# Squares of eight RMS norms around the output projection summed on GpSimd, with one product with the ones each

## The chip, the cores and the metric

One NeuronCore of a Trainium2 chip runs the kernel. The metric is the device time of one execution in microseconds, the median of several runs. The engines are TensorE (PE; its weight loads are PEld), VectorE (DVE), ScalarE (ACT), GpSimd (POOL) and SyncE (SP), each with an instruction queue that it works off in order; they hand over to each other by semaphores. Transfers are issued from the queues of SP, ACT and POOL.

## The reference

One decoder layer over 1024 prompt tokens and 32 sample tokens (8 sequences of 4, with a paged cache of 2048 positions each), float32, model width 1024:

```python
x = x + 0.5 * SwiGLU_1(rms_norm(x, g_ffn1))
q, k, v, logf, bg, uc = combined_projection(rms_norm(x, g_mix), w_in, b_f)
o_attn = forgetting_attention(q, k, v, logf)          # 8 heads of 64
conv_out = bg * short_conv(uc)                        # 512 channels
x = x + concat([rms_norm(o_attn, g_ao), rms_norm(conv_out, g_co)]) @ w_out
x = x + 0.5 * SwiGLU_2(rms_norm(x, g_ffn2))
y = rms_norm(x, g_final)

def rms_norm(x, g):
    return x * rsqrt(mean(x * x, axis=-1) + EPS) * g
```

## The kernel before, in words

Activations lie transposed: channels on the 128 partitions, tokens along the columns. The 1056 tokens are cut into four chunks `c` of 264 columns (`CH`). A tile of `[128, 4, 264]` holds four blocks of 128 channels of a chunk, so a norm over 512 channels has one such tile and a norm over 1024 channels two. Products are made in three float32r products of a high and a low part (`mm3`, lines 104 to 106).

An RMS norm (`norm`) needs, for each token, the sum of the squares over the channels, that is over the partitions and over the blocks. A product with a 128x128 matrix of ones gives that sum on all partitions at once, in a PSUM bank `ps`. `norm` has two ways to it:

- `stat_pe` (`short=True`): for each block ScalarE writes the squares of 128x264 to a small tile `sq` (tag `m1`, two buffers) and PE multiplies it with the ones in float32, adding up in `ps`. Four products for a norm over 512, eight for one over 1024.
- `stat_sum` (`short=False`): ScalarE squares a whole tile into `d` (tag `d`, one buffer), VectorE adds its halves (528 columns), then quarters (264 columns), and PE makes two float32r products of the sum's high and low part.

After that `rstd` makes 1/root of it (sqrt on ScalarE, line 170, with a table load where the table was another; reciprocal on VectorE, line 171), `scale` multiplies each block on VectorE (line 190), and `parts` makes the high part on ScalarE (line 193) and the low part on VectorE (line 194) that the next products read.

The norms that the change touches, in order of time:

- `conv_norm(0)` and `conv_norm(1)` within the attention, after its round 9 (`CONV_AT`), with banks of the attention's pool (`pco`). The order of the attention on PE is written out by hand: `front` (logits, lines 1126 to 1129, then softmax on VectorE and ScalarE), `middle` (transposes, line 1145), `back` (products with the values, line 1159; the result `at` is copied by ScalarE and VectorE, lines 1162 and 1163, and stored by a DMA from GpSimd's queue, line 1164).
- `attn_norm(0)`, `attn_norm(1)` and `conv_norm(2)` as hooks of the first half of the output projection, `project((0, 1), ...)`: it makes the products with the conv half (operand `opc`) for three blocks of the output, calls the hook, then makes those with the attention half (operand `op`) and adds `x` on VectorE (line 1263). At its end x goes to HBM by DMAs from GpSimd's queue (line 1266).
- `prepare(1)` as a hook of the second half, `project((2, 3), ...)`, and `prepare(2)` and `prepare(3)` after it. These are norms over 1024 channels; `halves` and `blocks` (lines 207 to 237) then make the operands for the next feed-forward stage, with a tile `d` of the same tag and one buffer. That stage begins with `plain` for three columns of weights, which reads operands of chunks 0 and 1 alone.

From the output projection on, a scheduler of the framework sets the order of each engine's instructions. `conv_norm(3)`, `attn_norm(2)`, `attn_norm(3)` and `prepare(0)` use `stat_sum`, before and after.

Of the kernel before, what the change touches and what calls it, by code (L numbers as in the profile page):

```python
# [8 lines left out]
F32 = mybir.dt.float32  # L9
# [3 lines left out]
AF = mybir.ActivationFunctionType  # L13
# [5 lines left out]
P = 128  # L19
D = 1024  # L20
# [11 lines left out]
CH = 264  # L32
# [26 lines left out]
G_F1, G_MIX, G_F2, G_FIN, G_AT, G_CO, CW = 0, 8, 16, 24, 32, 36, 40  # L59
# [3 lines left out]
class Step:  # L63
# [74 lines left out]
    def stat_pe(self, xs, ps):  # L138
        nc = self.nc
        for n, x in enumerate(xs):  # L140
            sq = self.tmp.tile([P, x.shape[1]], F32, tag="m1", bufs=2, name="sq")
            nc.scalar.activation(sq, x, AF.Square)
            nc.tensor.matmul(ps, self.ones, sq, start=n == 0, stop=n == len(xs) - 1)  # L143

    def stat_sum(self, ts, ps):

        nc = self.nc
        acc = None
        for t in ts:
            d = self.tmp.tile([P, 4, CH], F32, tag="d", bufs=1, name="d")  # L150
            nc.scalar.activation(d, t, AF.Square)
            nc.vector.tensor_add(d[:, 0:2], d[:, 0:2], d[:, 2:4])
            if acc is None and len(ts) > 1:
                acc = self.small("m5", self.nrs)
                nc.vector.tensor_add(acc, d[:, 0], d[:, 1])
                continue
            nc.vector.tensor_add(d[:, 0], d[:, 0], d[:, 1])
            if acc is None:
                acc = d[:, 0]
            else:  # L160
                nc.vector.tensor_add(acc, acc, d[:, 0])
        ah, al = (self.tmp.tile([P, CH], F32R, tag="m1", bufs=2, name=n) for n in ("ah", "al"))
        self.parts(ah, al, acc)
        nc.tensor.matmul(ps, self.ones_r, ah, start=True, stop=False)
        nc.tensor.matmul(ps, self.ones_r, al, start=False, stop=True)
# [8 lines left out]
    def norm(self, ts, col, n, ps=None, short=True, then=None):  # L174

        ps = self.bank() if ps is None else ps
        if short:
            self.stat_pe([t[:, k, :] for t in ts for k in range(4)], ps)
        else:
            self.stat_sum(ts, ps)  # L180
        rs = self.rstd(ps, n)
        for i, t in enumerate(ts):
            for k in range(4):
                c = col + 4 * i + k
                self.scale(t[:, k, :], t[:, k, :], self.prm[:, c:c + 1], rs)
                if then and k % 2:
                    then(i, k - 1)
# [241 lines left out]
def kernel(ctx: ExitStack, tc: tile.TileContext, io: dict):  # L429
    nc = tc.nc  # L430
    K = Step(tc, io)
# [6 lines left out]
    def pool(es, name, side="right", **kw):  # L438
        return es.enter_context(tc.tile_pool(name=name, bufs=1, side=side, reuse_waits="tile", **kw))
# [177 lines left out]
    with ExitStack() as es:  # L617
# [280 lines left out]
        def keep(g):  # L898

            po, M = ptr.tile([P, 512], F32, tag="tr", name="po"), Ms[g]  # L900
            for b4 in range(4):
                nc.tensor.transpose(po[:, P * b4:P * b4 + P], M[:, P * b4:P * b4 + P], ident)
            rows = po.rearrange("p (b a c q) -> p b a c q", b=4, a=NHP, c=4)
            for b4 in range(4):
                b = 4 * g + b4
                for hh in range(2):
                    pr = slice(HD * hh, HD * hh + HD)
                    nc.vector.tensor_copy(atS[pr, :, NT * b:NT * b + NT],
                                          rows[pr, b4, :, b4, NT * hh:NT * hh + NT])
# [176 lines left out]
    with ExitStack() as es:  # L1086
# [6 lines left out]
        def conv_load(c, pool_, tag, queue):  # L1093
            co = pool_.tile([P, 4, CH], F32, tag=tag, bufs=1, name="co")
            for t in range(4):
                queue.dma_start(co[:, t, :], co_d[t][:, c * CH:(c + 1) * CH])
            return co

        def conv_norm(c, co, ps=None):

            cs = slice(c * CH, (c + 1) * CH)
            K.norm([co], G_CO, 512, ps, short=c < 3)
            hi, lo = (opc.tile([P, 4, CH], F32R, tag=f"op{14 + 4 * c + j}", bufs=1, name="opc")
                      for j in range(2))
            K.parts(hi, lo, co)
            xo[c] = [(hi[:, k, :], lo[:, k, :]) for k in range(4)]
# [86 lines left out]
        for r in range(len(rounds)):  # L1193
            front(r + 1)
            middle(r)
            back(r - 1)
            if r == CONV_AT - 4:
                cos = [conv_load(c, K.tmp, f"co{c}", nc.gpsimd) for c in range(NCH // 2)]
            if r == CONV_AT:
                for c in range(NCH // 2):  # L1200
                    conv_norm(c, cos[c],
                              ptr.tile([P, 512], F32, tag="tr", bufs=3, name="pco")[:, :CH])
# [15 lines left out]
    def xtile(c):  # L1218

        ps, bufs = (xp0, 2) if c == 0 else (xp, 6)  # L1220
        return [ps.tile([P, 4, CH], F32, tag="x", bufs=bufs, name="x") for _ in range(2)]

    with ExitStack() as es:
        K.tmp = pool(es, "t3")
        xp = pool(es, "x3")
        xa, xs = [None] * NCH, [None] * NCH

        def attn_norm(c):

            cs = slice(c * CH, (c + 1) * CH)  # L1230

            a = op_l.tile([P, 4, CH], F32, tag=f"op{4 + c}", bufs=1, name="a")
            for t in range(NHP):
                nc.sync.dma_start(a[:, t, :], at_d[t][:, cs])
            K.norm([a], G_AT, 512, short=c < 2)
            hi, lo = (K.op_tile((16, 20, 24, 8)[c] + j) for j in range(2))
            K.parts(hi, lo, a)
            xa[c] = [(hi[:, k, :], lo[:, k, :]) for k in range(4)]

        def load_x(c):  # L1240
            xs[c] = xtile(c)
            for i in range(2):
                nc.sync.dma_start(xs[c][i], x_d[c][:, 4 * i:4 * i + 4, :])

        def project(cs, hooks):

            for (d0, d1), hook in zip(((0, 3), (3, 6), (6, KD)), hooks):
                os_ = {}
                for d in range(d0, d1):
                    ws = K.weight(io["w_out"][d, :, 512:], 512)  # L1250
                    for c in cs:
                        os_[d, c] = K.bank()
                        K.dot(os_[d, c], ws, xo[c], stop=False)
                hook()
                for d in range(d0, d1):
                    ws = K.weight(io["w_out"][d, :, :512], 512)
                    if d == 0:
                        for c in cs:
                            load_x(c)
                    for c in cs:  # L1260
                        o, x = os_[d, c], xs[c][d // 4][:, d % 4, :]
                        K.dot(o, ws, xa[c], start=False)
                        nc.vector.tensor_add(x, o, x)
            for c in cs:
                for i in range(2):
                    nc.gpsimd.dma_start(x2_d[c][:, 4 * i:4 * i + 4, :], xs[c][i])

        def prepare(c):
            K.norm(xs[c], G_F2, D, short=c > 0)
            K.halves(c // 2, c % 2, *xs[c], ops[c // 2])  # L1270

        def keep():
            K.plain_part([xp0.tile([P, 4, CH], F32R, tag="x", bufs=2, name="xb") for _ in range(2)], ops[0])

        def norms(c):
            conv_norm(c, conv_load(c, op_l, f"op{8 + c}", nc.sync))
            attn_norm(c)

        project((0, 1), (lambda: (attn_norm(0), attn_norm(1)), lambda: norms(2), lambda: norms(3)))
        project((2, 3), (lambda: prepare(0), lambda: prepare(1), lambda: K.blocks(0, ops[0], keep)))  # L1280
        w1, w3 = io["w1b"], io["w3b"]
        prepare(2)
        prepare(3)
        K.blocks(1, ops[1])
    K.after = None
# [126 lines left out]
```

## Time and profile before

| | |
|---|---|
| Median of three runs | 2158.63 us (2155.1 to 2159.55) |
| The profiled execution | 2156.09 us |
| Its span, first to last instruction | 2154.3 us |
| Mean granted clock of PE | 0.984 |
| PE busy | 2067.7 us, 96% |
| DVE busy | 1348.8 us, 63% |
| ACT busy | 866.0 us, 40% |
| POOL busy | 332.0 us, 15% |

All times within the execution are microseconds from its first instruction. PE's records overlap, since a product drains while the next one enters: the distance from start to start is what a product costs. Names at an arrow are tiles, without their buffer numbers: `ps<-sq,ones` is a product into a bank `ps` that reads `sq` and `ones`. A float32 product shows as two passes, so `x4` at line 143 is two products. The output projection runs from about 1311 to 1431.

### The profile page before, as it was taken

The numbers are of one execution on the slowest core, as the hardware profiler recorded it, in microseconds if no ns is written. First come the engines' busy times: TensorE is split into PE (matmuls) and PEld (weight loads), VectorE is DVE, ScalarE is ACT, GpSimd is POOL, SyncE is SP. The second block draws the span as 40 slices with busy tenths as digits, with TensorE's granted clock in tenths as the row PEclk, the third lists the DMA queues.
The fourth block names the chain that finished last, engine by engine and source line by source line (L and its number), as shares of the span: only waits on it lengthen the run. The fifth ranks groups of instructions, "written<-read, shape, count | busy, mean of one in ns | idle before, by whom it ended". The sixth has DMA issues, their size and how long they took to land.

```text
span 2154.3 us, 44569 instructions
## 1 busy us (share of the span) xinstructions
PE 2067.7 (96%) x17570; PEld 1981.6 (92%) x17570; DVE 1348.8 (63%) x2610; ACT 866.0 (40%) x1736; POOL 332.0 (15%) x487
## 2 busy tenths in 40 slices
PE   7999999999958999999999899999999999999998
PEld 7999999999957988888998677999999999999997
DVE  8877777776524664213225775897677677775354
ACT  6533333445312433222114764553333333454343
POOL 0011111110222021443432330001010111100000
PEclk9999999999978999999999999999999999999999
DMA  6222223257534668997976444332222222496353
GB/s 213 79 98 85 85 87 100 87 176 237 191 103 119 229 220 275 378 334 254 294 246 161 114 112 161 129 104 88 77 80 74 86 85 85 144 308 214 110 180 131
DMA packets 139618, 341.03 MB, mean 158 GB/s; under 512 B 30000, under 2 KB 46592, under 8 KB 137872
## 3 DMA queue, kind: packets, MB, share of 16 engines
q1 hardware_dynamic: 82704, 218.15, 31.6%
q0 software_dynamic: 28736, 88.50, 12.3%
q10 hardware_dynamic: 27968, 31.54, 4.8%
q8 instruction: 138, 2.26, 0.5%
q14 instruction: 72, 0.59, 0.1%
HBM read 279.75 MB, written 58.33 MB: 157 GB/s over the span
## 4 chain that ended last, share of the span: by engine, by line
PE 54%; DVE 4%; DMA 2%; ACT 1%; issue 1%; POOL 0%; SPq 0%; ACTq 0%; DVEq 0%; POOLq 0%
PE ps L105 12%; PE ps L104 12%; PE ps L106 11%; PE pg L104 4%; PE pg L105 4%; PE pg L106 4%; PE pv L886 1%; PE sc L843 1%; PE O L1159 1%; DMA wraw<-in_w_out 1%; PE ptp L1145 1%; PE S L1126 1%; PE ps L143 0%; PE S L1127 0%; ACT Pr L1134 0%
## 5 line engine op out<-in xcount | busy, mean ns | idle before, releaser
L105 PE MATMUL ps<-op,wh 128*128 128x264 f32 x2604 | 741.0, 285 | 0.7 <-DVE op L194 0.5
L106 PE MATMUL ps<-op,wl 128*128 128x264 f32 x2604 | 738.2, 284 | 0.0
L104 PE MATMUL ps<-op,wh 128*128 128x264 f32 x2604 | 737.4, 284 | 0.8 <-ACT op L193 0.4
L87 ACT CAST wh<-wraw 128x512 fp32r<-128x512 f32 x542 | 316.0, 601 | 491.3 <-PE ps L105 271.1
L104 PEld LDWEIGHTS ps<-op,wh 128*128 128x128 f32 x2604 | 489.5, 188 | 1.6 <-ACT op L193 0.8
L105 PEld LDWEIGHTS ps<-op,wh 128*128 128x128 f32 x2604 | 489.1, 188 | 1.8 <-DVE op L194 1.5
L106 PEld LDWEIGHTS ps<-op,wl 128*128 128x128 f32 x2604 | 490.2, 188 | 0.2
L89 DVE TENSOR_TENSOR wl<-wraw,wh 128x512 fp32r<-128x512 f32 x542 | 350.7, 663 | 201.8 <-ACT wh L87 176.5
L106 PE MATMUL ps<-h,wl 128*128 128x264 f32 x1408 | 405.3, 288 | 17.2 <-DVE wl L89 17.2
L105 PE MATMUL ps<-h,wh 128*128 128x264 f32 x1408 | 406.5, 289 | 14.3 <-DVE h L194 11.9
L104 PE MATMUL ps<-h,wh 128*128 128x264 f32 x1408 | 408.2, 290 | 4.5 <-ACT wh L87 4.5
L106 PEld LDWEIGHTS ps<-h,wl 128*128 128x128 f32 x1408 | 271.2, 193 | 18.7 <-DVE wl L89 18.6
L105 PEld LDWEIGHTS ps<-h,wh 128*128 128x128 f32 x1408 | 270.8, 192 | 15.2 <-DVE h L194 15.0
L104 PEld LDWEIGHTS ps<-h,wh 128*128 128x128 f32 x1408 | 271.2, 193 | 5.2 <-ACT wh L87 5.0
L104 PE MATMUL pg<-XH,wh 128*128 128x352 f32 x576 | 189.8, 329 | 1.7 <-issue 1.7
L106 PE MATMUL pg<-XH,wl 128*128 128x352 f32 x576 | 185.0, 321 | 0.3 <-issue 0.3
L105 PE MATMUL pg<-XL,wh 128*128 128x352 f32 x576 | 184.7, 321 | 0.0
L87 ACT CAST wh<-s 128x512 fp32r<-128x512 f32 x176 | 108.2, 618 | 120.3 <-PE ps L105 110.2
L89 DVE TENSOR_TENSOR wl<-s,wh 128x512 fp32r<-128x512 f32 x176 | 120.6, 690 | 24.2 <-ACT wh L87 18.9
L327 POOL DMA_DIRECT2D h_d<-t x79 | 42.8, 542 | 602.1 <-DVE t L326 598.0
L104 PEld LDWEIGHTS pg<-XH,wh 128*128 128x128 f32 x576 | 108.0, 188 | 18.4 <-issue 18.1
L106 PEld LDWEIGHTS pg<-XH,wl 128*128 128x128 f32 x576 | 108.1, 188 | 0.8 <-issue 0.8
(276 smaller groups left out, 2586.4 us busy)
## 6 DMA issues: line engine op xcount, KB each, us to landing
wraw<-in_w2a SPq DMA_DIRECT2D x48, 512.0 KB
wraw<-in_w2b SPq DMA_DIRECT2D x48, 512.0 KB
h_d<-t POOLq DMA_DIRECT2D x176, 132.0 KB
h<-h_d SPq DMA_DIRECT2D x88, 264.0 KB
kvraw<-in_kc SPq DMA_DIRECT2D x64, 256.0 KB
kvraw<-in_vc SPq DMA_DIRECT2D x64, 256.0 KB
wraw<-in_w1a SPq DMA_DIRECT2D x28, 512.0 KB
wraw<-in_w3a SPq DMA_DIRECT2D x28, 512.0 KB
```

The lines of the kernel that those rows point to most:

```text
L87: nc.scalar.copy(wh, x)
L89: nc.vector.tensor_sub(wl, x, wh)
L104: nc.tensor.matmul(ps, w[0], x[0], start=start, stop=False)
L105: nc.tensor.matmul(ps, w[0], x[1], start=False, stop=False)
L106: nc.tensor.matmul(ps, w[1], x[0], start=False, stop=stop)
L327: nc.gpsimd.dma_start(h_d[2 * p + 1][:, f, :], t)
L843: nc.tensor.matmul(ps[quarter(hp)], QZ[:, g, hp, 32 * b4:32 * b4 + 32], raw[:, :, hp * P:hp * P + P], start=b4 == 0, stop=b4 == 3)
L886: nc.tensor.matmul(pv[quarter(hp), cs], PT[:, 4 * j + s, quarter(hp)], raw[:, s, hp * P:hp * P + P], start=j == 0 and s == 0, stop=False)
L1126: nc.tensor.matmul(S[:, k0:k1], QA[:, qs], KA[:, k0:k1], start=True, stop=False)
L1145: nc.tensor.transpose(pt_[:, j * P:(j + 1) * P], Pr[:, (j0 + j) * P:(j0 + j + 1) * P], ident)
L1159: nc.tensor.matmul(O[HD * b + q:HD * b + q + 32], V[:, j, c0 + q:c0 + q + 32], pt[:, j, :], start=j == 0, stop=j == n)
```

## The change

A third way, `stat_pool`, takes the place of `stat_pe` in the eight norms. It squares a whole tile of four blocks at once on ScalarE into `d`, adds on GpSimd in float32 (halves, then quarters; with two tiles also the second tile's sum to the first's, `acc`), and makes one float32 product with the ones. The norm of chunk 1 at the kernel's start stays with `stat_pe`.

```diff
+    def stat_pool(self, ts, ps):
+
+        nc = self.nc
+        acc = None
+        for t in ts:
+            d = self.tmp.tile([P, 4, CH], F32, tag="d", bufs=1, name="d")
+            nc.scalar.activation(d, t, AF.Square)
+            nc.gpsimd.tensor_add(d[:, 0:2], d[:, 0:2], d[:, 2:4])
+            if acc is None and len(ts) > 1:
+                acc = self.tmp.tile([P, CH], F32, tag="m1", bufs=2, name="acc")
+                nc.gpsimd.tensor_add(acc, d[:, 0], d[:, 1])
+                continue
+            nc.gpsimd.tensor_add(d[:, 0], d[:, 0], d[:, 1])
+            if acc is None:
+                acc = d[:, 0]
+            else:
+                nc.gpsimd.tensor_add(acc, acc, d[:, 0])
+        nc.tensor.matmul(ps, self.ones, acc, start=True, stop=True)
+
...
-        if short:
+        if short == "pool":
+            self.stat_pool(ts, ps)
+        elif short:
             self.stat_pe([t[:, k, :] for t in ts for k in range(4)], ps)
...
-            K.norm([co], G_CO, 512, ps, short=c < 3)
+            K.norm([co], G_CO, 512, ps, short="pool" if c < 3 else False)
...
-            K.norm([a], G_AT, 512, short=c < 2)
+            K.norm([a], G_AT, 512, short="pool" if c < 2 else False)
...
-            K.norm(xs[c], G_F2, D, short=c > 0)
+            K.norm(xs[c], G_F2, D, short="pool" if c > 0 else False)
```

The lines of the changed kernel lie 19 to 21 further on: 151 is the new square, 152, 155, 157 and 161 the adds, 162 the product, 1185 the store of `at`, 1287 that of x.

What it does to the order, at two places. The first is `prepare(2)` and `prepare(3)` at the end of the output projection. On PE, before (the first row ends the projection, `op_17905` and `op_17906` belong to `plain` of the next stage):

```order
L106 MATMUL ps<-op_17709,wl 128x264
L143 MATMUL ps<-sq,ones 128x264 x9
L104 MATMUL ps<-op_17905,wh 128x264
L105 MATMUL ps<-op_17906,wh 128x264
L106 MATMUL ps<-op_17905,wl 128x264
L104 MATMUL ps<-op_17905,wh 128x264
L143 MATMUL ps<-sq,ones 128x264 x2
L105 MATMUL ps<-op_17906,wh 128x264
L143 MATMUL ps<-sq,ones 128x264 x2
L106 MATMUL ps<-op_17905,wl 128x264
L143 MATMUL ps<-sq,ones 128x264 x2
L104 MATMUL ps<-op_17905,wh 128x264
```

and now (`op_17870` and `op_17871` are the same two operands):

```order
L106 MATMUL ps<-op_17674,wl 128x264
L162 MATMUL ps<-acc,ones 128x264 x2
L104 MATMUL ps<-op_17870,wh 128x264
L105 MATMUL ps<-op_17871,wh 128x264
L106 MATMUL ps<-op_17870,wl 128x264
```

Sixteen products, the last seven of them strewn among products of the next stage, became two that stand side by side ahead of that stage. On GpSimd's queue at the same place (lines 152 to 161 are the adds, `x_d` the stores of x at the end of the projection's second half):

```order
L1287 DMA x_d_81<-x 128x1056
L1287 DMA x_d_82<-x 128x1056
L152 TENSOR_TENSOR d<-d 128x528
L1287 DMA x_d_81<-x 128x1056
L1287 DMA x_d_82<-x 128x1056
L155 TENSOR_TENSOR acc<-d 128x264
L152 TENSOR_TENSOR d<-d 128x528
L157 TENSOR_TENSOR d<-d 128x264
L161 TENSOR_TENSOR acc<-acc,d 128x264
L152 TENSOR_TENSOR d<-d 128x528
L155 TENSOR_TENSOR acc<-d 128x264
L152 TENSOR_TENSOR d<-d 128x528
```

The stores of the first halves of x of chunks 2 and 3 stand ahead of `prepare(2)`'s first add, those of the second halves between its first and second add; before, the four stores were alone there.

The second place is round 9 of the attention, `conv_norm(0)` and `conv_norm(1)`. GpSimd's queue before (`at_d` are the stores of the attention's results, `vt`, `KA` and the like loads for the next heads):

```order
L1164 DMA at_d_115<-at 64x256 x2
L1164 DMA at_d_116<-at 64x256
L926 DMA vt<-v_d_109 128x1024
L921 DMA KA<-k_d_103 64x1024 x2
L921 DMA QA<-q_d_95 64x1024
```

and now:

```order
L1185 DMA at_d_115<-at 64x256 x2
L152 ISA
L152 TENSOR_TENSOR d<-d 128x528
L1185 DMA at_d_116<-at 64x256
L157 TENSOR_TENSOR d<-d 128x264
L947 DMA vt<-v_d_109 128x1024
L152 TENSOR_TENSOR d<-d 128x528
L157 TENSOR_TENSOR d<-d 128x264
L942 DMA KA<-k_d_103 64x1024 x2
L942 DMA QA<-q_d_95 64x1024
```

The first norm's two adds stand on both sides of the third store, the second norm's after the load of `vt`; ahead of the first add stands an instruction that was not there. On PE the eight products of these two norms became two in the same place.

## Rows read from the trace of the kernel before

**Rows 1.** Page, engines: busy us, share of the span, instructions.

```profile
PE 2067.7 (96%) x17570; PEld 1981.6 (92%) x17570; DVE 1348.8 (63%) x2610; ACT 866.0 (40%) x1736; POOL 332.0 (15%) x487
```

**Rows 2.** Timeline, prepare(1): start, us, engine, line, out<-in, count [idle before <-releaser].

```profile
1381.21 0.42 ACT L142 ACTIVATE sq<-x 128x264 f32<-128x264 f32 x1 [0.20 <-PE ps L164]
...
1395.15 0.28 PE L106 MATMUL ps<-opc,wl 128*128 128x264 f32 x1
1395.27 1.05 PE L143 MATMUL ps<-sq,ones 128*128 128x264 f32 x4
1395.97 0.48 PE L104 MATMUL ps<-op,wh 128*128 128x264 f32 x1
1396.28 0.28 PE L105 MATMUL ps<-op,wh 128*128 128x264 f32 x1
...
1400.90 0.29 PE L105 MATMUL ps<-op,wh 128*128 128x264 f32 x1
```

**Rows 3.** Timeline, conv norms 0 and 1 in the attention.

```profile
1202.54 0.53 POOL L1164 DMA_DIRECT2D at_d<-at  x1 [3.26 <-DVE at L1163]
...
1204.62 1.16 PE L143 MATMUL pco<-sq,ones 128*128 128x264 f32 x4
...
1207.04 0.53 POOL L1164 DMA_DIRECT2D at_d<-at  x1 [3.96 <-DVE at L1163]
...
1211.47 0.59 PE L1126 MATMUL S<-KA,QA 128*128 128x512 f32 x1
```

**Rows 4.** Timeline, attention norms 0 and 1.

```profile
1320.23 3.06 PE L143 MATMUL ps<-sq,ones 128*128 128x264 f32 x10
...
1326.64 0.29 PE L106 MATMUL ps<-opc,wl 128*128 128x264 f32 x1
...
1329.53 1.21 DVE L194 TENSOR_TENSOR op<-a,op 128x1056 fp32r<-128x1056 f32 x1
```

**Rows 5.** Timeline, conv norm 2.

```profile
1345.20 1.05 PE L143 MATMUL ps<-sq,ones 128*128 128x264 f32 x4
...
1347.82 0.29 PE L104 MATMUL ps<-op,wh 128*128 128x264 f32 x1
```

**Rows 6.** Timeline, prepare(2) and prepare(3).

```profile
1420.07 4.35 PE L143 MATMUL ps<-sq,ones 128*128 128x264 f32 x14
...
1420.44 1.25 DVE L194 TENSOR_TENSOR op<-d,op 128x1056 fp32r<-128x1056 f32 x1
...
1423.50 0.53 POOL L1266 DMA_DIRECT2D x_d<-x  x1 [18.89 <-DVE x L1263]
...
1430.93 0.28 PE L106 MATMUL ps<-op,wl 128*128 128x264 f32 x1
```

**Rows 7.** Line 143: PE passes, duration ns min/median/max, first and last start.

```profile
L143 PE MATMUL ps<-sq,ones x88: 383/386/807, 12.2 to 1430.6; 128*128 128x264 f32 x88
```

**Rows 8.** Groups by shape: count | busy us, mean ns | idle before, releasers.

```profile
L170 ACT ACTIVATE rs<-ps,eps 128x264 f32<-128x264 f32 x22 | 10.5, 478 | 4.7 <-issue 1.6 <-PE ps L143 1.2 <-PE ps L350 0.8
L151 ACT ACTIVATE d<-x 128x1056 f32<-128x1056 f32 x8 | 8.7, 1083 | 4.9 <-DVE m L155 1.7 <-DMA x<-in_xT 1.6 <-issue 1.5
L170 ACT ACT_TABLE_LOAD x6 | 7.7, 1283 | 0.1
...
L152 DVE TENSOR_TENSOR d<-d 128x528 f32<-128x528 f32 x11 | 7.7, 701 | 8.0 <-ACT d L151 8.0
L157 DVE TENSOR_TENSOR d<-d 128x264 f32<-128x264 f32 x7 | 2.9, 420 | 0.0
...
L629 POOL MEMSET QZ<- 128x1280 f32 x1 | 1.2, 1184 | 0.0
L634 POOL MEMSET VS<- 128x512 f32 x1 | 0.5, 544 | 0.0
```

**Rows 9.** Stretches: length, busy of PE, PEld, DVE, ACT, POOL, granted clock, DMA, GB/s.

```profile
1217.00:1218.00 1.00, 0.00 (x0) 0.00 (x0) 1.00 (x1) 1.00 (x4) 0.39 (x1) 1.00 0.94 184
...
1220.00:1221.00 1.00, 1.00 (x8) 0.79 (x5) 1.00 (x2) 0.67 (x2) 0.00 (x0) 0.50 1.06 229
```

## The prediction

> **What bounds the kernel.** I read the page's engine table first: TensorE (PE) is busy 96% of the span [rows 1]. So a microsecond counts where PE stands still or does work that could go away. Then I read, place by place, what the squares cost PE. The stretch from the first product with the ones to where the ordinary products run undisturbed again, less 0.12 us for each ordinary one in between (their distance, 1395.15 to 1395.27 [rows 2]), is PE's loss to a norm. Two products back to back take 0.70 us, 0.35 each, and the ordinary one behind them 0.31 instead of 0.12 [rows 2]; the rest is waiting, since a square can be written only when a product has freed one of two buffers.
>
> - A, conv norms 0 and 1 inside the attention: 1204.62 to 1211.47, nothing in between, 6.85 us [rows 3].
> - B, attention norms 0 and 1: 1320.23 to 1326.64, five ordinary ones, 5.8 us [rows 4].
> - C, conv norm 2: 1345.20 to 1347.82, three, 2.26 us [rows 5].
> - E, prepare(1): 1395.27 to 1400.90, ten, 4.4 us [rows 2].
> - D, prepare(2) and (3): 1420.07 to 1430.93, eight, 9.9 us [rows 6].
>
> Together 29.2 us. That is the most that a free sum could give back, less 8 times 0.35 us. What matters is whether the new sum is ready when PE arrives, for PE takes its instructions in order.
>
> **The change, part by part.** *Removed:* 44 squares of 264 columns and 44 fp32 products, each two passes of 0.386 us [rows 7]. *Added:* 11 squares of 1056 columns at 1.083 us [rows 8], 8 products, 25 adds on GpSimd (11 of 528 columns, 14 of 264), and one ISA instruction ahead of the first add. ScalarE gets less to do (44 squares against 11), so only order and waits matter there. One load of x goes ahead of one weight load in SyncE's queue; both are issued long before use, nothing.
>
> *Price of an add.* No GpSimd arithmetic is in the trace. From below: the same add on VectorE (DVE), 0.70 and 0.43 us [rows 8]. From above: GpSimd's own memsets take 1.184 us for 1280 columns and 0.544 for 512 [rows 8], so 0.83 ns a column and 0.12 us fixed; an add reads two streams and writes one, and three passes make 1.44 and 0.78 us. Two passes make 1.00 and 0.56. I take the middle of two and three, 1.2 and 0.67 us, because the memsets are rows of the engine itself. The Trainium skill speaks against the change here (GPSIMD Engine Reference, Elementwise — side-by-side cycle accounting): an fp32 add of 2048 columns takes 4497 ns on GpSimd, 1.96 times VectorE; scaled by columns, an estimate of 1.16 and 0.58 us, which would make the sum below 4.3 us instead of 5.2 (no row here shows such an add).
>
> *Gains.* At C and E the rows of the order show the adds far ahead of PE. At E ScalarE wrote a first square of this norm at 1381.21 [rows 2], so its x was there 14 us before PE came; the new chain, two squares and five adds with prices below, is 7 us long, and PE meets a finished sum: 4.4 less 0.35 and the slow follower's 0.19, **+3.9 us**. At C the same way 2.26 less 0.54, **+1.7 us**. If that cover were gone, the sum at E would be the wait that takes the place of the old one, up to the 7 us less the 4.4.
>
> *A.* The second add of conv norm 0 stands behind a store of `at` that ends at 1207.57 [rows 3]. Then add 0.67, product (0.70 to its end: four passes take 1.05 [rows 2], less 0.35), sqrt 0.48 [rows 8], and only then the square of norm 1, because there is one buffer `d`: 1.08, adds 1.2 and 0.67, product 0.35. With 0.1 us for each hand-over PE gets to the logits at about 1213.1, against 1211.47: **-1.6 us** (-0.6 with VectorE's prices, -2.1 with three passes). I let it reach the end of the attention in full.
>
> *B.* Here too product 2 waits for product 1, sqrt, square and adds in a row. PE waits about 1 us for the first sum and over 4 us for the second, and is through at about 1326.3. It has 24 ordinary products (2.9 us) to do before it needs the operand whose last part VectorE starts at 1329.53 and ends 1.2 us later [rows 4]. That part comes some 0.5 us sooner; the clock (below) can eat that: **0** (-1.5 to +0.5).
>
> *D.* This decides. The two products stand next to each other, ahead of all products of the next stage, which need neither. Both sums go through the one `d`, which is also the `d` of blocks(0): its last reader starts at 1420.44 and takes 1.25 us [rows 6]. From PE's arrival (0 = 1420.07): `d` free 1.6; square to 2.7; add 4.0; then on GpSimd's queue two x stores of 0.54 us that wait for the last x and, before, were issued from 1423.50 [rows 6], to 5.1; add 5.75; square 6.95; adds 8.25, 8.95, 9.65; square of norm 3 10.85; adds 12.15, 12.85; square 14.05; adds 15.35, 16.05, 16.75; second product at 16.85, ordinary work 0.54 later at 17.4. Before, the loss was 9.9: **-7.5 us** (-4.1 with VectorE's prices, -9.1 with three passes). The next stage's other engines can't give it back; it is PE-bound.
>
> *Clock.* After PE had done nothing from about 1215.3 to 1218.6, the granted clock stood at 0.50 (1.2 instead of 2.4 GHz) from 1220 to 1223 [rows 9], 3.4 us in all with the slices around. A stall of 15 us at D should bring the same: half of 3.4, **-1.7 us** (0 if the gaps around the first product count as work).
>
> Sum: -1.6 + 0 + 1.7 + 3.9 - 7.5 - 1.7 = **5.2 us slower**. The profiled execution took 2156.09 us, 2.5 under the median of the runs, so it would be 2161.3; beside the median of 2158.63 it is **2163.8 us**.
>
> **Rivals.**
>
> 1. *Not slower: the adds cost what VectorE takes, and the clock holds.* A -0.6, B +0.5, C and E +5.6, D -4.1: 1.4 us faster, 2157.2. For it: GpSimd is idle in the whole stage but for the x stores. Against: its memsets [rows 8] run at one column in 0.83 ns with one stream. The place is D. With the clock falling the sum crosses zero just under those prices, at about 0.65 and 0.40; without it at about 0.85 and 0.50. To be faster than what a measurement can tell (0.2%, 4.3 us) the two sums at D must nearly be done on PE's arrival, which the shared `d` forbids.
> 2. *The ISA instruction takes time.* It stands before the first add, at A, after the store at 1202.54. GpSimd has then 4.0 us until the next store [rows 3], and the add needs 1.2, so 2.8 us are covered; a load like ScalarE's table load (1.28 us [rows 8]) would cost nothing, and each microsecond over 2.8 moves A by one. By the Trainium skill (GPSIMD Engine Reference, Instruction dispatch) the first call after a library load pays some 6 us; no row here shows it; it would give 3.2 us more, 2167. As a rival, from the rows: a load of twice to four times the table load's length, up to 2.3 us more, 2166.
> 3. *Adds and VectorE's two-operand instructions block each other.* At D the first two adds run beside such instructions of 1.25 us, those of norm 3 beside a row of scalings of 0.49. If four wait out half of 1.25 and four half of 0.49, it is 3.5 us, 2167. That is the rule of the Trainium skill (SBUF — State Buffer, Who interferes with whom): one lock, the later one waits for the whole instruction. The trace before has no GpSimd read to show it.
>
> That the change doesn't do what it says is excluded by the order: 44 products became 8.
>
> **How the numbers follow.** Forecast (2160.5 to 2166) 0.44, rival 1 0.22, rival 2 0.15, rival 3 0.17, rest 0.02. Rival 1 lies within 0.2% (2154.3 to 2162.9) but for its tail, and the lower third of the forecast does too: same 0.30; tail of rival 1: faster 0.06; the rest, slower 0.64. The range goes from rival 1 (2157) to rivals 2 and 3 together with three-pass adds (2172). The forecast's own range is 2160 to 2167.
>
> **What would show it.** Right: at D one wait of PE of some 15 us for a GpSimd add, ending the first row of ordinary products at half clock; at A PE waiting twice, for GpSimd both times, and resuming logits 1 to 3 us later relative to the round before; at C and E single products without a wait. The GpSimd adds themselves, by their spacing: 1.2 and 0.67. Wrong: adds under 0.7 us, PE not waiting at D, or a first add at A that ends after 1207 (then rival 2).

## The result, and the profile after

| | before | after |
|---|---|---|
| Median | 2158.09 us (2155.09 to 2162.32, six runs) | 2177.39 us (2174.37 to 2180.29, six runs) |
| Ratio | | 1.0084, 95% interval 1.0067 to 1.0101 |
| The profiled execution, its span | 2156.09, 2154.3 | 2180.22, 2178.5 |
| Mean granted clock of PE | 0.984 | 0.974 |

The change made the kernel slower by about 18 us (14 to 22), where 5.2 was forecast: the sign was right, the size outside the range (2157 to 2172). The page's engine line, against [rows 1]:

```profile
PE 2055.5 (94%) x17498; PEld 1976.4 (91%) x17498; DVE 1356.1 (62%) x2610; ACT 857.2 (39%) x1703; POOL 359.5 (17%) x512
```

PE works 12 us less than before, as it should with 36 products fewer, and the span is 24 us longer. So most of the loss is time in which PE stands still. The waits of PE from 1200 to 1460, the three largest (engine, line, what it waited for: us in total, times, longest us):

```profile
PE ps L162 <- POOL acc L161: 21.4, 2, 15.0
PE pco L162 <- POOL d L157: 7.5, 2, 3.8
PE ps L162 <- POOL d L157: 4.9, 2, 4.0
```

The new products alone (line 162) wait 34 us: 21.4 at D, 7.5 at A, 4.9 at B, and not at C or E.

Where does that stand against what the old way lost? The ordinary products of PE (those without the ones) are equally many in both traces from the attention's first logits on. So the start of the n-th of them, less that of the n-th before, tells by how much the program is behind at that place. The table is worked out so from PE's timeline, at points between A, B, C, E and D where PE's order is the same; the step from one column to the next is what the place in its head cost (the time of the point before, in the kernel before, stands in brackets).

| kernel | 40th product (1168.9) | ahead of A (1204.4) | first logits after A (1211.5) | A done (1240.8) | B done (1343.0) | C done (1357.6) | ahead of E (1395.2) | E done (1411.7) | D done (1445.9) |
|---|---|---|---|---|---|---|---|---|---|
| after | 1.2 | 7.6 | 9.9 | 12.8 | 15.0 | 13.5 | 13.1 | 9.1 | 24.1 |

From D on the 24.1 stay as they are to the end. So A cost 5.2 us, B 2.2, D 15.0; C gave 1.6 and E 4.0, and another 0.4 came back between C and E. Together that is 16.5 us slower, within the 14 to 22 of the runs. The 7.6 ahead of A come before the first added instruction. Most of them arise between the 40th product and A, where kernels whose attention is that of before move by chance too, from 1.3 us less to 6.1 more (below). So they are put down to chance and left out of the sum.

The timeline at A (start, us, engine, line, out<-in, count [idle before <-releaser]), against [rows 3]:

```profile
1210.11 0.53 POOL L1185 DMA_DIRECT2D at_d<-at  x1 [3.74 <-DVE at L1184]
1210.74 1.34 POOL L152 TENSOR_TENSOR d<-d 128x528 f32<-128x528 f32 x1
1214.61 0.55 POOL L1185 DMA_DIRECT2D at_d<-at  x1 [2.54 <-DVE at L1184]
1215.18 0.76 POOL L157 TENSOR_TENSOR d<-d 128x264 f32<-128x264 f32 x1
1215.99 0.91 PE L162 MATMUL pco<-d,ones 128*128 128x264 f32 x2 [3.73 <-POOL d L157]
...
1217.32 1.07 ACT L151 ACTIVATE d<-co 128x1056 f32<-128x1056 f32 x1
...
1219.84 0.81 POOL L157 TENSOR_TENSOR d<-d 128x264 f32<-128x264 f32 x1
1220.71 1.25 PE L162 MATMUL pco<-d,ones 128*128 128x264 f32 x2 [3.80 <-POOL d L157]
1221.38 1.00 PE L1147 MATMUL S<-KA,QA 128*128 128x512 f32 x1
```

The first add ends at 1212.1, but the second stands behind the store of `at`, which waits until 1214.61. Only after the first norm's product and root does ScalarE square the second `co` (1217.32), because there is one `d`. PE waits 3.73 and 3.80 us and begins the logits at 1221.38. The stretches around it (length, busy of PE, PEld, DVE, ACT, POOL, granted clock, DMA, GB/s), against [rows 9]:

```profile
1216.00:1220.00 4.00, 0.90 (x2) 0.29 (x2) 2.51 (x3) 1.45 (x2) 1.88 (x3) 0.55 0.36 131
1220.00:1224.00 4.00, 3.29 (x9) 2.49 (x10) 2.86 (x5) 1.45 (x2) 0.65 (x1) 0.50 0.00 0
1224.00:1228.00 4.00, 3.99 (x36) 2.97 (x38) 3.97 (x6) 1.31 (x3) 2.73 (x6) 0.67 0.33 102
```

The granted clock falls to 0.50, and is still 0.67 in the mean of 1224 to 1228, where PE is busy again.

D, the same view as [rows 6]:

```profile
1433.56 1.25 DVE L215 TENSOR_TENSOR op<-d,op 128x1056 fp32r<-128x1056 f32 x1
1434.91 1.08 ACT L151 ACTIVATE d<-x 128x1056 f32<-128x1056 f32 x1 [1.15 <-DVE op L215]
...
1438.46 1.78 POOL L155 TENSOR_TENSOR acc<-d 128x264 f32<-128x264 f32 x1
...
1444.41 1.25 PE L162 MATMUL ps<-acc,ones 128*128 128x264 f32 x2 [15.05 <-POOL acc L161]
1448.04 5.38 DVE L211 SCALAR_TENSOR_TENSOR x<-x,prm,rs 128x264 f32<-128x264 f32 x8
...
1451.97 1.25 PE L162 MATMUL ps<-acc,ones 128*128 128x264 f32 x2 [6.32 <-POOL acc L161]
```

PE arrives at 1429.36 and waits 15.05 us for the first sum; the first square begins only at 1434.91, when VectorE's last reader of `d` (1433.56 and 1.25 us) lets go of the buffer. From there to the second product it is 17.06 us, one step after another. The adds themselves (the view of lines 152 and 157: count, ns min/median/max, first and last start):

```profile
L152 POOL TENSOR_TENSOR d<-d x11: 1289/1301/2110, 1210.7 to 1448.8; 128x528 f32<-128x528 f32 x11
L152 POOLq MODIFY_POOL_CONFIG  x2: 42/42/42, 1210.6 to 1210.7; - x2
L157 POOL TENSOR_TENSOR d<-d x8: 738/808/828, 1215.2 to 1450.2; 128x264 f32<-128x264 f32 x8
```

An add of 528 columns takes 1.30 us in the median, one of 264 0.81. The longest of the former, 2.11, ran beside VectorE's work. The instruction ahead of the first add shows as two of 0.042 us.

### The profile page after: what moved, and what is told of

Read it like the earlier page. It is cut to its first block, busy times and chain, and to the rows that moved or that the text cites. A ratio compares the mean times of both kernels' runs of the same rounds, so it can differ in the third digit from the quotient of the medians.

```text
span 2178.5 us, 44438 instructions
## 1 busy us (share of the span) xinstructions
PE 2055.5 (94%) x17498; PEld 1976.4 (91%) x17498; DVE 1356.1 (62%) x2610; ACT 857.2 (39%) x1703; POOL 359.5 (17%) x512
## 4 chain that ended last, share of the span: by engine, by line
PE 53%; DMA 2%; DVE 2%; issue 2%; ACT 1%; POOL 1%; SPq 0%; ACTq 0%; DVEq 0%; POOLq 0%
PE ps L104 12%; PE ps L105 12%; PE ps L106 12%; PE pg L104 4%; PE pg L106 4%; PE pg L105 4%; PE O L1180 1%; PE sc L864 1%; PE pv L907 1%; PE ptp L1166 1%; PE S L1147 1%; DMA wraw<-in_w_out 1%; PE S L1148 1%; DVE x L211 1%; DMA KA<-k_d 1%
## 5 line engine op out<-in xcount | busy, mean ns | idle before, releaser
L105 PE MATMUL ps<-h,wh 128*128 128x264 f32 x1408 | 405.7, 288 | 16.4 <-DVE h L215 12.8
L105 PEld LDWEIGHTS pg<-XL,wh 128*128 128x128 f32 x576 | 108.9, 189 | 0.0
```

What stands on the lines that cost most here:

```text
L105: nc.tensor.matmul(ps, w[0], x[1], start=False, stop=False)
```

## The experiments

Twelve kernels, each with a profile, in three groups with the kernel before among them. The table continues the one above, with the ratio to before in the same group. A stands for the step from "ahead of A" to "A done", D for that from "E done" to "D done"; a minus is a gain.

| kernel | ratio, interval | 40th product | ahead of A | A | B | C | E | D |
|---|---|---|---|---|---|---|---|---|
| after | 1.0084 (1.0067 to 1.0101) | 1.2 | 7.6 | 5.2 | 2.2 | -1.6 | -4.0 | 15.0 |
| e1_ce | 1.0000 (0.9985 to 1.0014) | 2.7 | 6.5 | 2.6 | 1.3 | -1.6 | -4.0 | 5.6 |
| e2_d | 1.0043 (1.0024 to 1.0063) | 1.5 | 1.9 | 0.1 | 0.0 | 0.0 | 0.1 | 11.6 |
| e3_ab | 1.0028 (1.0012 to 1.0044) | 0.5 | 3.7 | 5.5 | 1.2 | 0.0 | 0.5 | 0.0 |
| e4_own | 1.0064 (1.0046 to 1.0083) | 1.2 | 0.3 | 4.9 | 3.4 | -1.5 | -4.0 | 10.2 |
| e5_afill | 1.0017 (1.0000 to 1.0034) | 2.7 | 6.6 | 0.6 | 0.0 | 0.0 | 0.7 | 0.0 |
| e6_late | 1.0043 (1.0025 to 1.0062) | 5.1 | 4.4 | 4.0 | 3.6 | -1.5 | -4.0 | 3.9 |
| e7_best | 1.0029 (1.0005 to 1.0052) | 6.4 | 10.5 | 2.4 | 1.3 | -1.6 | -4.0 | 4.7 |
| e8_latepe | 1.0012 (0.9996 to 1.0029) | 5.7 | 4.4 | 0.2 | -0.1 | 0.0 | 0.1 | 2.2 |
| e9_room | 0.9996 (0.9980 to 1.0012) | -0.3 | 0.7 | 0.8 | 0.2 | -0.5 | -0.9 | -2.3 |
| e10_ce_nosub | 1.0005 (0.9986 to 1.0024) | 2.7 | 8.8 | 0.1 | 1.3 | -1.6 | -4.0 | 3.8 |
| e11_before_nosub | 0.9987 (0.9972 to 1.0002) | -4.2 | -3.1 | 0.8 | 0.0 | 0.0 | 0.3 | 0.1 |
| e12_d_dve | 1.0061 (1.0039 to 1.0083) | -0.5 | 1.8 | 0.8 | 0.0 | 0.0 | 0.8 | 12.1 |

The steps of kernels that leave a place as before scatter by 0.0 to 0.8, at A once by 2.6 and once by 2.4. (The 1.3 at B of e1_ce, e7_best and e10_ce_nosub is no scatter; see e1.) Between the 40th product and A they move by chance too: with the attention of before, e10_ce_nosub loses 6.1 us there and e8_latepe gains 1.3.

**e1 to e3: the change in three parts.**

- e1_ce: `conv_norm(2)` and `prepare(1)` with `"pool"`, the rest as before.
- e2_d: `prepare(2)` and `prepare(3)` with `"pool"`, the rest as before.
- e3_ab: `conv_norm(0)`, `(1)` and `attn_norm(0)`, `(1)` with `"pool"`, the rest as before.

> The new sum only at C (conv norm 2) and E (prepare(1)), where the changed kernel's PE gains 1.6 and 4.0 us; A, B and D as before. Theory 1 (PE's loss at each place is its own): 5.6 us faster than before, 2152.5. Theory 2 (behind E, VectorE's queue is full and the weight loads come when they come, so that PE, 4 us sooner at D, meets squares that are not sooner): D's loss grows from 9.9 to about 13.5 us, and the kernel is only 1.5 to 2 us faster, 2156.5.

> The new sum only at D (prepare(2) and (3)). As predicted blind (a chain of 15.3 us that starts 1.6 us after PE's arrival, clock 1.7): 9.2 us slower than before, 2167. Theory 2 (in the changed kernel, which loses 15.0 us at D, the start is 4.1 us later only because E's gain brought PE there sooner): without that gain 15.0 less 4.0, some 11 us slower, 2169, and PE stands about 19 us from its arrival to the second product's end. If the start is late for another reason: 15 us slower, 2173.

> The new sum only at A and B (conv norms 0 and 1, attention norms 0 and 1). As predicted blind: 1.6 us slower (A) and 0 (B), 2160. By the changed kernel's trace: A 5.2, B 2.2, together 7.4 us slower, 2165.5; of A's 5.2 some 2.5 to 3 are a stretch at half clock behind the two waits. If PE's later start of the attention in the changed kernel's profile (4.7 us before the first add) belongs to the change and not to chance, another 4 to 5 us: 2170.

C and E alone gain 1.6 and 4.0 us, to the tenth what the changed kernel shows, and D, where nothing was changed, loses 5.6 more than before. The lead over the point "B done" is gone (10.4 there, 10.4 at "D done"). The ratio of 1.0000 (3 us either way) excludes theory 1's 5.6 us. The mechanism of theory 2 holds; its gain of 1.5 to 2 us is not excluded by the ratio, but the places show less, since B and the clock (both below) take their part. The timeline of e1_ce tells how:

```profile
1406.48 0.62 ACT L87 CAST wh<-wraw 128x512 fp32r<-128x512 f32 x1 [5.01 <-DMA wraw<-in_w_out]
...
1408.74 0.48 ACT L189 ACTIVATE rs<-ps,eps 128x264 f32<-128x264 f32 x1
1409.48 1.80 DVE L190 RECIPROCAL rs<-rs 128x264 f32<-128x264 f32 x1
...
1429.67 0.73 ACT L142 ACTIVATE sq<-x 128x264 f32<-128x264 f32 x2
1430.14 6.38 PE L143 MATMUL ps<-sq,ones 128*128 128x264 f32 x14 [4.28 <-ACT sq L142]
```

```profile
1430.00:1431.00 1.00, 0.86 (x2) 0.76 (x3) 1.00 (x2) 0.40 (x2) 0.00 (x0) 0.50 0.00 0
```

PE's product with the sum of prepare(1) starts at 1404.00. The root of it stands on ScalarE behind two casts of weights, the first of which waits 5.01 us for its load, and starts at 1408.74. VectorE follows at 1409.48 and has work without a pause of over 0.3 us to 1433; the squares of D stand behind that work and behind more casts. Two of them were written ahead, into the two small buffers; the third begins at 1429.67. PE, 4 us ahead, waits 4.28 for it, to 1430.14. Behind the wait the granted clock is 0.50 until 1435, and the five products from there on take 1.1 us longer than before. So the 5.6 us are the wait and the half clock. Before, the root came at 1400.98, right behind the products.

B, where nothing was changed either, loses 1.3 us, in e7_best and e10_ce_nosub too. What they have in common is C's new sum. Its first add starts at 1335.07 in e1_ce and runs beside the four scalings with which VectorE ends the norm ahead of it, `attn_norm(0)`. Those scalings before:

```profile
1326.19 1.70 DVE L190 SCALAR_TENSOR_TENSOR a<-a,prm,rs 128x264 f32<-128x264 f32 x4
```

and in e1_ce:

```profile
1335.26 3.12 DVE L211 SCALAR_TENSOR_TENSOR a<-a,prm,rs 128x264 f32<-128x264 f32 x4
```

They take 1.42 us more, and PE gets the operand made from them that much later. In the changed kernel C's adds run beside the scalings of `attn_norm(1)`, and PE waits for that operand, which it does not in e3_ab:

```profile
1343.37 3.27 DVE L211 SCALAR_TENSOR_TENSOR a<-a,prm,rs 128x264 f32<-128x264 f32 x4
...
1347.80 0.39 PE L104 MATMUL ps<-op,wh 128*128 128x264 f32 x1 [1.02 <-ACT op L214]
```

So C's gain of 1.6 us is paid for at B with 1.3 us in e1_ce and 1.0 in the changed kernel (2.2 there against e3_ab's 1.2).

D alone costs 11.6 us, as theory 2 said. The timeline of e2_d there:

```profile
1423.67 1.08 ACT L151 ACTIVATE d<-x 128x1056 f32<-128x1056 f32 x1 [0.94 <-DVE op L215]
1433.17 1.25 PE L162 MATMUL ps<-acc,ones 128*128 128x264 f32 x2 [10.98 <-POOL acc L161]
1440.75 1.25 PE L162 MATMUL ps<-acc,ones 128*128 128x264 f32 x2 [6.33 <-POOL acc L161]
```

The first square starts 1423.67, which is 1.6 us after PE's arrival (1420.07 and 1.97 later [rows 6]), as the prediction had it, and the second product stands 17.1 us after that, where 15.3 were forecast. In the changed kernel the chain is as long (17.06), and its start 5.5 us after PE's arrival instead of 1.6.

A and B alone cost 5.5 and 1.2 us, and the ratio (6 us, interval 2.6 to 9.5) bears it out. The attention's later start showed half (3.2). In kernels without the change there it is as large, so it is put down to chance.

**e4: a tile for each square.**

```diff
...
-            d = self.tmp.tile([P, 4, CH], F32, tag="d", bufs=1, name="d")
+            d = q.tile([P, 4, CH], F32, tag=tag, bufs=1, name="d")
...
```

`q` and `tag` name an operand tile that is idle then, another one for each square of A, B and D.

> The changed kernel, with a tile of its own for each square at A, B and D (operand tiles that are idle then), so that no square waits for another norm or for blocks(0). If the shared buffer costs most: the second wait goes at A (3.8 us and part of the half clock, 5 us in all), at B (4.0 us) and at D (7 us, and the start moves to the last x), together 15 to 18 us faster than the changed kernel, about 2161. If the price of the adds and PE's order cost most, and the buffer little: under 6 us faster, over 2171. D alone should still lose 5 to 8 us against before, since the last x comes from VectorE 6 to 7 us after PE's arrival.

Only 4.3 us of the 18 came back by the ratios (1.0084 and 1.0064, whose intervals overlap). At D the start of the chain is no longer `d`, but the last x:

```profile
1211.27 1.25 PE L162 MATMUL pco<-d,ones 128*128 128x264 f32 x2 [1.65 <-POOL d L157]
1211.94 1.00 PE L1147 MATMUL S<-KA,QA 128*128 128x512 f32 x1
...
1432.91 1.11 POOL L1287 DMA_DIRECT2D x_d<-x  x2 [13.08 <-DVE x L1284]
1440.18 2.13 PE L162 MATMUL ps<-acc,ones 128*128 128x264 f32 x4 [16.80 <-POOL acc L161]
```

The stores of x at 1432.91 wait for VectorE's last addition, 9.5 us after PE's arrival at 1423.38; the squares of the second halves come behind that, and PE still stands 16.80 us. A is the surprise: the second wait falls from 3.80 to 1.65 us, the logits start at 1211.94, 0.5 us later than before's, and A costs 4.9 us all the same. The stretches behind:

```profile
1209.00:1213.00 4.00, 2.35 (x6) 1.49 (x6) 1.80 (x1) 0.48 (x1) 2.22 (x3) 0.52 0.42 122
...
1217.00:1221.00 4.00, 3.48 (x35) 2.51 (x34) 1.78 (x4) 3.93 (x6) 2.46 (x5) 0.50 0.98 240
...
1225.00:1229.00 4.00, 3.47 (x16) 3.23 (x17) 3.94 (x10) 3.87 (x12) 1.06 (x2) 0.50 0.07 16
```

The clock stays at 0.50 to 0.52 over all of it, also in the stretches between. (Here ScalarE also loads its tables twice more, since the two roots stand apart.) B costs 3.4 us, more than with one buffer: the second wait fell from 3.98 to 1.80 us as expected, but PE then waits 2.29 and 0.87 us for the operand, since VectorE now makes the second norm's reciprocal ahead of the first norm's scalings.

**e5: idle products in A's waits.** This is A alone, with eight products into the same bank ahead of each new one:

```diff
+        for _ in range(8): nc.tensor.matmul(ps, self.ones, ts[0][:, 0], start=True, stop=True)
         nc.tensor.matmul(ps, self.ones, acc, start=True, stop=True)
```

> The new sum only at A, and ahead of each of its two products eight idle products (2.8 us) into the same bank, where PE would only wait; the result is unchanged. If the half clock behind the two waits is what costs at A (the clock theory): the granted clock stays at 1.00 around A, and A's loss falls from 4.6 to 5.2 us to about 2; 2 us slower than before. If A's loss is the wait itself and the order that follows it: A still loses 4.5 to 5, or more, since the idle products may come too late.

```profile
1211.21 3.83 PE L162 MATMUL pco<-co,ones 128*128 128x264 f32 x16
1215.00 0.71 PE L163 MATMUL pco<-d,ones 128*128 128x264 f32 x2
...
1219.53 0.71 PE L163 MATMUL pco<-d,ones 128*128 128x264 f32 x2 [0.25 <-POOL d L157]
```

```profile
1212.00:1216.00 4.00, 4.00 (x19) 3.14 (x18) 1.08 (x3) 2.31 (x6) 1.79 (x3) 1.00 0.07 16
1216.00:1220.00 4.00, 3.75 (x18) 2.91 (x16) 3.65 (x4) 1.20 (x2) 2.10 (x2) 1.00 0.47 135
```

The logits begin 1.8 us later than before's in the table's measure (6.6 to 8.4), nearly as much as in the changed kernel (2.3). But the granted clock is 1.00 up to 1225 (and 0.84 and 0.74 in the two stretches of 4 us behind, where before has 0.84 and 0.73 from 1217), and A costs 0.6 us in the end instead of 5.2 to 5.5. So by these profiles most of A's loss was the clock behind the waits, not the waits. The ratio (0 to 7 us slower) is too wide to tell e5_afill from e3_ab.

**e6 and e7: work ahead of D's products.** To e4_own the first column of `plain` is moved ahead of `prepare(2)`; e7_best has that, but A and B as before.

```diff
+        for f in range(1):
+            K.plain(w1, w3, (f,), 0, ops[0], h2_d, tags=("m5", "m5", "m1"))
         prepare(2)
         prepare(3)
...
-    for f in range(N0B):
+    for f in range(1, N0B):
```

`tags` gives the moved column's results `m` the buffers `m5` and `m1`; `m1` has two buffers, and `acc` (or `sq` before) uses the same two.

> As with a tile of its own for each square, and in addition the first column of plain (96 products, 11.5 us) ahead of prepare(2) and (3) in the program. If D's loss is PE standing in order before sums that come 17 us after its arrival (the last x, then squares and adds): PE now waits some 5.5 us instead of 16.8 behind 11.5 us of work, D's offset against before goes from -10.2 to +4, and the kernel from 13 us slower to 0 to 2 us faster or slower. If VectorE's queue takes plain's work ahead of the last x, the sums come as much later as PE is later: 8 us or more slower than before.

> The new sum at C, E and D alone, the squares of D in tiles of their own, the first column of plain ahead of prepare(2) and (3); A and B as before. By the place by place losses: C 1.6, E 4.0, D 4: some 9 us faster than before, 2150. If E's gain is lost again wherever PE next meets VectorE's queue: D +0, 2 to 4 us faster at most.

In e6_late PE has 11.5 us of work in hand and still waits:

```profile
1435.52 1.11 POOL L1287 DMA_DIRECT2D x_d<-x  x2 [14.26 <-DVE x L1284]
1438.80 1.30 POOL L152 TENSOR_TENSOR d<-d 128x528 f32<-128x528 f32 x1 [2.17 <-ACT d L151]
...
1446.15 1.25 PE L162 MATMUL ps<-acc,ones 128*128 128x264 f32 x2 [7.57 <-POOL acc L161]
1449.10 1.25 PE L162 MATMUL ps<-acc,ones 128*128 128x264 f32 x2 [1.70 <-POOL acc L161]
...
1478.77 0.59 PE L104 MATMUL ps<-op,wh 128*128 128x264 f32 x1 [3.15 <-ACT s L286]
```

The stores of x, at 1435.52, are a little sooner than in e4_own, seen from PE's place (6.7 us behind before here, 3.1 there), but the first add comes 3.3 us behind them: ScalarE loads a table and works off `plain`'s first result ahead of the squares. The adds into `acc` also wait, 0.36 us for the store of `m` and 0.80 for PE, since `m` holds one of their two buffers. PE waits 7.57 and 1.70 us, D costs 3.9, and behind it 4.0 more are lost (10.5 behind at "D done", 14.5 at the end), with one wait of 3.15 us for ScalarE's result of the next column. By the ratios e6_late is 4.5 us better than e4_own, within their intervals. In e7_best the gain at E is gone once more: 4.7 us are lost at D and 5.4 more behind it. 9 us faster was one theory's sum and 2 to 4 faster the other's; it is 6 us slower (1 to 11), so both missed.

**e8: the same move alone.** The edit is that of e6, made to the kernel before.

> The kernel before, with only the first column of plain ahead of prepare(2) and (3): none of the new sums. If before's loss at D (9.9 us) were mostly the wait for the last x: it falls to the products' 5.6 us, 4 us faster. If it is the two small buffers that square and product pass to and fro (1.2 us for two): the same 9.9 us, later; within 1 us of before.

D costs 2.2 us more, against a 4 us gain in the one theory and nothing in the other; the ratio can't tell it from no change. The edit itself has a part in this: `m` of the moved column holds one of the squares' two buffers until its store has landed, and ScalarE's fourth square waits for that:

```profile
1440.88 0.73 ACT L142 ACTIVATE sq<-x 128x264 f32<-128x264 f32 x2 [0.92 <-DMA h_d<-m]
```

Up to there PE waits 0.97, 0.51, 0.51 and 0.63 us for one square at a time, 2.6 in all. So no gain of 4 us is seen, but how much of before's loss at D is the two buffers, this run does not show.

**e9: room for the squares, without GpSimd.**

```diff
...
+            d = q.tile([P, 4, CH], F32, tag=tag, bufs=1, name="d")
+            nc.scalar.activation(d, t, AF.Square)
+            for k in range(4):
+                nc.tensor.matmul(ps, self.ones, d[:, k, :], start=n == k == 0, stop=n == len(ts) - 1 and k == 3)
...
```

> No GpSimd, no VectorE: at B, C, E and D the square of a whole tile of four blocks goes at once into an operand tile that is idle then, and PE makes the same four or eight fp32 products from it as before; A as before. If before's losses are squares and products passing two small buffers to and fro: each place falls towards 0.35 us a product, B 5.8 to 3.8, C 2.3 to 1.6, E 4.4 to 3.0, D 9.9 to 8.8; 5 us faster at most, 2 to 3 if E's share is lost again at D. If before's losses are VectorE's last x and the order of PE: within 1 us of before.

C, E and D gain 0.5, 0.9 and 2.3 us, B nothing instead of 2.0, and 1.6 are lost between C and E, where nothing was changed. So the passing to and fro of the buffers is worth something at three places, but the ratio, 0.9996, is no change that can be told.

**e10 and e11: less work for VectorE.** Left out are the three subtractions of `blocks(0)`, in e1_ce and in the kernel before.

> As with the new sum at C and E alone; left out are the three subtractions of blocks(0) that go through d (3.75 us of VectorE between E and D; T1, T2 and T4 are then wrong). If VectorE's queue sets when the squares of D can begin: D's loss falls by 3 to 4 us against the same kernel with them (from 15.5 to about 12), and the kernel is 3 to 4 us faster than that one. If D waits for something else (weights, ScalarE): no change.

> The kernel before without the same three subtractions. There PE reaches D 4 us later, while the queue of VectorE is as far; its squares start 0.7 us after PE's arrival, so at most 1 to 2 us of D's 9.9 can go. If it gains 3 to 4 us too, VectorE's queue bounds this stage in the kernel before as well, and E's gain could never have shown.

3.75 us of VectorE's work less bring D 1.8 us (5.6 to 3.8), and before's D nothing. PE still waits 3.39 us for the third square, and the clock falls behind that wait as in e1_ce. What holds the square shows on ScalarE:

```profile
1424.01 1.14 ACT L87 CAST wh<-wraw 128x512 fp32r<-128x512 f32 x2 [7.21 <-DMA wraw<-in_w1b]
...
1428.66 0.73 ACT L142 ACTIVATE sq<-x 128x264 f32<-128x264 f32 x2
```

The squares stand behind casts, one of which waited 7.21 us for the next stage's weights to land. So these 3.75 us of VectorE's work account for a third of D's 5.6 us, and ScalarE's casts and the weights' loads ahead of the squares for more; what sets the pace of those loads there was not tried.

**e12: D's adds on VectorE.**

```diff
-            nc.gpsimd.tensor_add(d[:, 0:2], d[:, 0:2], d[:, 2:4])
+            nc.vector.tensor_add(d[:, 0:2], d[:, 0:2], d[:, 2:4])
...
```

The other adds of `stat_pool` likewise.

> The new sum at D alone with its ten adds on VectorE in place of GpSimd. If the price of GpSimd's adds (1.30 and 0.8 us against 0.70 and 0.43) and VectorE's waits beside them are what costs: the chain of 17.0 us falls to 12 to 13 and D's loss against before from 11.6 to about 7. If the single buffer and the place in VectorE's queue cost most: 10 us or more.

```profile
1431.68 1.25 PE L162 MATMUL ps<-acc,ones 128*128 128x264 f32 x2 [8.33 <-DVE acc L161]
1442.60 1.25 PE L162 MATMUL ps<-acc,ones 128*128 128x264 f32 x2 [9.66 <-DVE acc L161]
```

PE waits 8.33 and 9.66 us. The first sum is sooner than on GpSimd (10.98 us of waiting in e2_d), the second later, since its adds stand in VectorE's queue between the scalings of the first norm. D costs 12.1 against 11.6: what the shorter adds save, their place in VectorE's queue takes again. The single buffer was left as it was; what it costs without that queue, this run does not show.

## Why the prediction was wrong

Of the 11.3 us between the forecast (5.2) and the sum of the places (16.5), D has 5.8, A 3.6 and B 2.2; C and E together came out as forecast, within 0.4. By the terms of the prediction:

- **C and E, +1.7 and +3.9: right** as what PE gains at these two places (1.6 and 4.0). The step that failed is that they stand in the sum as if they were kept. C's adds cost 1.0 to 1.3 us at B, by making VectorE's scalings there longer. E's gain was lost at D, all of it in e1_ce; in the changed kernel D costs 15.0 instead of e2_d's 11.6, so 3.4 of some 6 were lost.
- **D, -7.5: the mechanism was right, the size was not.** "`d` free 1.6" was taken from rows of before as a distance from PE's arrival. VectorE's queue didn't move with PE, so it was 5.5: 4 us. The chain from there, forecast at 15.3, took 17.1: adds of 1.30 and 0.74 to 0.83 us for 1.2 and 0.67, and one of 1.78 beside VectorE. Both together are 5.7 of the 5.8 us by which D (15.0 with the clock) missed the 9.2. The sign "one wait of PE of some 15 us" was met by luck: by the prediction's own chain PE would wait some 9.7 us and then 6.5, as in e2_d (10.98 and 6.33); the changed kernel's 15.05 holds the 4 us that were not forecast.
- **A, -1.6: the wait was right** (logits 2.3 us later, 1.8 in e5_afill), the term for the clock was missing. It was priced at D alone, at 1.7; at A it cost some 4.6, since e5_afill, with the clock up, loses 0.6 instead of 5.2. What it cost at D was not taken apart.
- **B, 0:** 2.2, and 1.2 in e3_ab. The forecast end of the second product was about right against before's, but the operand did not come 0.5 us sooner: VectorE's four scalings took 2.46 us beside the second norm's adds instead of 1.70. And the granted clock fell there too (0.69 and 0.50 from 1331 to 1339 in e3_ab, where PE waits for no operand). The 1.0 more in the changed kernel is C's.
- **Rival 1** (adds at VectorE's price): out by the rows, 1.30 and 0.74 to 0.83 us against 0.70 and 0.42 ([rows 8]; the prediction has 0.43). e12_d_dve has that price and costs 12.1 at D, though there the adds stand in VectorE's queue.
- **Rival 2** (the ISA instruction): out. Two instructions of 0.042 us; the first add starts 0.1 us after the store ends (1210.11 and 0.53). The Trainium skill (GPSIMD Engine Reference, Instruction dispatch) would have had some 6 us there; no run shows it, and the first add (1.34 us) is about as long as the others (1.30).
- **Rival 3** (adds and VectorE block each other): seen, and it was looked for at D alone. An add of 528 columns of C took 2.11 us beside VectorE, one of 264 1.78 at D, and VectorE's eight scalings at 1448.04 took 5.38 us, where before they took 3.31 (1403.70). The rule of the Trainium skill (SBUF — State Buffer, Who interferes with whom) agrees with these rows in that both sides get slower; whether one waits for the whole of the other they don't show. On PE's path it cost 1.0 us at D and, through the scalings, another 1.0 at B.
- **The price of an add:** the middle of two and three memset passes, 1.2 and 0.67, was below the 1.30 and 0.81 of the rows. The estimate from the Trainium skill's figure (GPSIMD Engine Reference, Elementwise — side-by-side cycle accounting), 1.16 and 0.58, was further off, above all for the smaller add: two adds of 264 columns (1.48 to 1.62) take 0.2 to 0.3 us more than one of 528 (1.30), a fixed part that scaling by columns leaves out.

What stays open: how the 3.4 us at D divide between VectorE's queue, the weights' loads and the clock, and how much of B is the clock; none was tried alone. No version beat before.

## What to carry to other kernels

A gain on the bounding engine counts only up to the next place where it meets another engine's queue: before adding it to the sum, look whether that queue is full (VectorE was, from 1409 on) and whether its work hangs on the gain at all; "so long after PE's arrival" holds only while both move together. A reduction that replaces many small products by one turns a stream that PE can begin on into a chain that it can only wait for, so what matters is the chain's length from the last input, through each shared buffer, and what stands behind the product in PE's order. A gain also has to be set against what the new work does to engines that it runs beside: here the adds of one norm made the scalings of another longer. And a wait of some us on PE costs more than itself where the clock falls behind it: price that at every wait, not at the longest alone.

## What the runs showed of the hardware

- With two waits of 3.7 and 3.8 us and one product between, the granted clock was 0.55, 0.50 and 0.67 in the three stretches of 4 us from 1216. In e4_own it was 0.52 to 0.50 from 1209 to 1229, and the 0.5 us by which PE was late became 4.9. With idle products in the waits (e5_afill) it stayed at 1.00 to 1225. At D of the changed kernel it was 0.50 from 1432 on and 0.59 in the mean of 1452 to 1456.
- VectorE lost most of what the GpSimd adds beside it took: 2.07 us on eight scalings (5.38 less 3.31), beside which GpSimd's three adds took 2.92. Four scalings of 1.70 us took 2.46 to 3.27 beside adds.
- With the same attention, the stretch of 36 us ahead of A differs by 7 us from profile to profile.
